# Values of the strided attention groups: token order and a DRAM round trip in place of a stationary operand of every fourth column

## The chip, the cores and the metric

The kernel runs on one core of a Trainium2 chip. TensorE (PE) multiplies, with a queue of its own for loading the stationary operand (PEld); VectorE (DVE), ScalarE (ACT) and GpSimd (POOL) do the elementwise work, and SyncE (SP) issues nearly all transfers. The metric is the device time of one execution in microseconds. Before the change it is 3572.5 us, the median of three runs between 3571.23 and 3573.5 us.

## The reference

The program is a stack of four layers over 512 tokens of 1024 features (with 256 context tokens in the first two), all in float32: a neighbourhood attention layer, a gated scan layer, and two hybrid layers, which the change touches. A hybrid layer projects the normed tokens to queries, keys and values of three attention groups of four heads (head size 128), to a retention branch and to gates. Group 0 attends the last 128 tokens; groups 1 and 2 attend tokens at distances that are multiples of 4 and of 16:

```python
ATT_PATTERNS = ((128, 1), (512, 4), (2048, 16))
...
def dilated_window_attention(q, k, v, window, dil):
    """Keys are gathered by stride: the sequence is split into dil residue classes, each attended with a
    banded (current + previous block) causal window."""
...
    def to_sub(t):
        t = t.astype(jnp.float32).reshape(B, L, dil, G, Dh).transpose(0, 2, 3, 1, 4)
```

The groups' outputs are weighted by their softmax denominators, gated, merged with the retention branch and projected back.

## The kernel before, in words

Every float32 product is made of three float32r products (`mm3`, L142 to L148): the operands are cut into a high and a low part, and high x high, high x low and low x high are added in PSUM. Weights come as 512 KB tiles `wraw` (three buffers, L121), which SP loads; a pair of tiles `whi`, `wlo` (six buffers each) holds 512 columns' worth of parts, the high ones made by ACT (L132), the low ones by POOL and DVE in turn (L135). A chunk of 256 weight columns for all 1024 input features is 1 MB: two `wraw` tiles, four pairs.

In a hybrid layer (`b2_layer`, L1360) `H` holds the normed tokens as two parts with features on the partitions. `dense` (L1322) gives 128 columns for all tokens with the weights stationary (128 x 512 outputs). `dense_v` (L1330) gives values, with tokens on the partitions: the tokens' parts are stationary and 256 weight columns move (128 x 256 outputs). It goes token tile after token tile; a tile takes 8 row blocks x 3 = 24 products, a call 96. With `classes`, for groups 1 and 2, tile `t` is made of every fourth token from `t` on, and the stationary operand is taken with that stride:

```python
            for k in range(KT):
                lh = [x[:, t::4] for x in H.row(k)] if classes else H.tok(k, t)
                S.mm3(p[:, u * 256:(u + 1) * 256], lh, W(k), k == 0, k == KT - 1)
```

So the stationary columns are 16 bytes apart. Two calls with `classes` follow each other ahead of heads 0 and 2 of each hybrid layer, for groups 1 and 2 of two heads at once: eight calls, 768 products. A call without `classes` stands in the retention's values (`b2_retain`, four a layer, with `parts`) and in group 0's for heads 2 and 3. ACT copies each pair of token tiles from PSUM to `V` (L1351).

`b2_attend` (L1411) then makes the queries and keys of what groups are left, the scores and exponentials, exchanges maxima and sums between the two token orders by way of DRAM (`stats`, L1455 and L1456), makes the first products of the next head (`between`), and then the outputs: probabilities are transposed (`pt`, L1480), copied (`PT`), and multiplied by `V` (`o`, L1494), first group 0 (`lay` 0), then groups 1 and 2. These last instructions lie between products of the next head in TensorE's order. A scheduler that works from priorities and modelled costs sets the order on each engine; each engine works its list in that order, and SP waits in its list for a buffer to come free.

Of the kernel before, what the change touches and what calls it, by code (L numbers as in the profile page):

```python
# [9 lines left out]
F32 = mybir.dt.float32  # L10
# [4 lines left out]
AF = mybir.ActivationFunctionType  # L15
# [3 lines left out]
D = 1024  # L19
KT = 8  # L20
# [5 lines left out]
KBASE = (0, 8, 24, 32)          # first key column of each 16-column query block  # L26
BOFF = (16, 8, 8, 0)            # its offset in the wide bias table
BVAR = (0, 1, 1, 2)

# columns of the packed per-feature vectors  # L30
# [10 lines left out]
# 2 pi in parts of 8 bits, whose products with small integers are exact  # L41
# [12 lines left out]
class Acts:  # L54
    """Activations with features on the partitions, as float32r parts [hi, lo]: 512 latent tokens and,
    in smaller tiles, 256 context tokens."""
# [18 lines left out]
class Prog:  # L75
# [14 lines left out]
    # ---------------------------------------------------------------- helpers  # L90
# [8 lines left out]
    def t2(self, name="t", n=512, dt=F32):  # L99
        """a short-lived tile of up to 2 KB a partition"""  # L100
        return self.sb.tile([128, n], dt, name=name, tag="t2", bufs=6)
# [7 lines left out]
    def weights(self, srcs, kt, own=None):  # L109
        """Loads float32 columns and cuts each value into two float32r parts whose sum it is.  # L110
        Returns a function of the row block that gives the two parts."""
# [27 lines left out]
    def wcols(self, w, c0, n, k0=0, kt=KT):  # L139
        """[128, kt, n] view of columns c0.. of a [K, N] weight."""  # L140
        return w[k0 * 128:(k0 + kt) * 128, c0:c0 + n].rearrange("(k p) n -> p k n", p=128)

    def mm3(self, out, lh, rh, first, last):
        """out (+)= (lh0+lh1).T @ (rh0+rh1), the product of the low parts being below float32."""
        nc = self.nc
        nc.tensor.matmul(out, lh[0], rh[0], start=first, stop=False)  # L146
        nc.tensor.matmul(out, lh[0], rh[1], start=False, stop=False)  # L147
        self.lastmm = nc.tensor.matmul(out, lh[1], rh[0], start=False, stop=last)  # L148

    def rsqrt(self, ss, scale, n, name="rs"):  # L150
        """(ss*scale + EPS) ** -0.5 on a few columns: Newton's steps from a first guess by the exponent."""
# [11 lines left out]
    def row_rstd(self, x, room):  # L163
        """(mean of squares + EPS) ** -0.5 of the rows of a token tile, half a row at a time; room: for the squares"""
# [12 lines left out]
    def rstd(self, ss, n, d):  # L177
        """(ss / d + EPS) ** -0.5 of sums of d squares, by GpSimd"""
# [6 lines left out]
    # ---------------------------------------------------------------- constants  # L185
    def setup(self):
# [11 lines left out]
        # the gated scan's lower bounds of the forget gates, and one less them  # L198
# [6 lines left out]
        # silu of the three conditioning vectors; c and c_ctx interleaved for the first products  # L205
# [7 lines left out]
    # ---------------------------------------------------------------- modulation vectors  # L213
    def ada_first(self):
        """shift and scale of the first norm for c and c_ctx, as columns: A = g * (1 + scale), shift"""
# [68 lines left out]
def ffn(S, l, xs, xout, more):  # L284
    """xout(t) is the residual tile that gets gate * swiglu(h); the last two of six tiles are the context's"""
# [16 lines left out]
    def dense(f):  # L302
        """a and u columns of feature tile f"""
# [18 lines left out]
    for gi, gn in enumerate(groups):  # L322
        gts = []
        for f in range(f0, f0 + gn):
# [5 lines left out]
            if l == 0:      # from columns first to rows first  # L330
# [12 lines left out]
            # a gate that this layer itself waits for comes at once  # L343
# [58 lines left out]
# which 1024 columns of a modulation matrix, and the names its vectors go by  # L402
# [3 lines left out]
def gemv_jobs(S, pool, wname, layer, part, vecs, ps, tag):  # L406
    """vec @ w + b for one 1024-column part, 256 columns a step, as a row in DRAM: S.rows[part, layer, v]."""
# [35 lines left out]
def gemv_rows(S, pool, wname, layer, part, ps, tag):  # L443
    """The same for c and c_ctx on the tensor engine, where other work leaves it idle."""
# [33 lines left out]
def gemv_flush(S, pool, ps, tag, after):  # L478
    """the sums over the partitions of the steps so far, behind other products so that no engine waits for them"""
# [21 lines left out]
def gate_bcast(S, part, layer, v, pool=None, tag="gate", bufs=2):  # L501
    """a modulation row on every partition"""
# [6 lines left out]
def mod_cols(S, sh, sc, g, layer, v):  # L509
    """(g * (1 + scale), shift) as columns"""  # L510
# [10 lines left out]
def residual_add(S, x, p, gate, c0, n):  # L521
    """x[:, c0:c0+n] += gate * p"""
# [6 lines left out]
def out_product(S, w, tok, xs, gates, own, tags, after=None):  # L529
    """xs[t] += gate * (h @ w): the first half of the columns for all the token tiles at once, row block by row  # L530
    block; then the other half a token tile after the other"""
# [25 lines left out]
def norm_block(S, xs, A, sh, rows, room, banks, hold=(), both=False, split=True):  # L557
    """h = x / rms(x) * A + sh of token tiles as two parts, with features on the partitions; rows(k): where
    row block k goes; room(): space for the scaled rows of a tile; banks: tags of the PSUM tiles to turn it in"""
# [43 lines left out]
def grid_rows(ap, t):  # L603
    """rows of a [512, D] array for the token tile of grid columns 16t.., column-major"""
# [16 lines left out]
def l0_start(S):  # L621
    nc, sb, ps, I = S.nc, S.sb, S.ps, S.I
    # residual rows, column-major grid order for the latent tokens
# [20 lines left out]
def na_heads(S, na, hT, jobs):  # L644
    """Head pair after head pair. The order of the instructions is the one they are written in: three phases of
    the attention, each a step behind the one before, with the products of the next heads between them."""
# [45 lines left out]
    # the products of the first heads come before the attention  # L692
# [63 lines left out]
class Feed:  # L756
    """A sequence of products, and of what follows from them some time of products later."""
# [8 lines left out]
    def then(self, lag, fn, cost=0.0):  # L766
        """after the last product and lag"""
# [11 lines left out]
def feed_weights(S, F, src, me):  # L779
    """the parts of a weight chunk, two row blocks at a time, as soon as the last one's products let them go"""  # L780
# [140 lines left out]
def o_row(oT, pr, lat):  # L921
    """outputs of a head pair, [feature, token]"""
# [5 lines left out]
def split_rows(S, oR, oT, pr):  # L928
    """the outputs of a head pair as two parts"""
# [7 lines left out]
def na_scores(S, na, st, g, h, b, qk, mask):  # L937
    """a step of the attention: softmax of 16 columns' queries, or of 128 context tokens"""
# [24 lines left out]
def na_max(S, me, h, b):  # L963
    """minus the maxima; the scores are negative ones"""
# [62 lines left out]
# ---------------------------------------------------------------- gated scan layer  # L1027
# [3 lines left out]
def view(t, off, dims):  # L1031
    """free-dimension pattern over a tile"""
# [80 lines left out]
def hg_qg(S, hT, w, c0, tag):  # L1113
    """silu of two heads' 256 columns from c0 on"""
# [16 lines left out]
def hg_head(S, hT, w, h, V, lb, om, masks, q, reads):  # L1131
# [4 lines left out]
    # forget gates; index 0 is the backward direction in f, the forward one in K  # L1136
# [26 lines left out]
    # Q: q (1 - lb) times the decays; the keys stay without their (1 - lb)  # L1163
# [10 lines left out]
    for li, m in enumerate(LEVELS):  # L1174
# [9 lines left out]
        # decays over whole blocks join  # L1184
# [19 lines left out]
    # states between the 128-token blocks: keys with tokens on the partitions, then k.T @ v  # L1204
# [41 lines left out]
def hg_read(S, h, on, g):  # L1246
    """output of a head, normed and gated, [feature, token]"""
# [16 lines left out]
# ---------------------------------------------------------------- hybrid layers  # L1264
# [3 lines left out]
def b2_tables(S):  # L1268
    """attention masks, and cos and sin of the rotary angles, [angle, position]"""
# [52 lines left out]
def dense(S, W, H, j):  # L1322
    """features on the partitions: 128 columns of a weight chunk for all the tokens"""
# [6 lines left out]
def dense_v(S, W, H, classes=False, parts=False, rows=False):  # L1330
    """tokens on the partitions: 256 columns of a weight chunk as [token, tile, column]; classes: tile r
    holds every fourth token from r on; parts: as two parts; rows: row block by row block"""
    V = [S.sb.tile([128, 4, 256], F32R if parts else F32, name="V", tag="hC", bufs=4) for _ in range(1 + parts)]
    if rows:
# [426 lines left out]
```

## Time and profile before

| What | Value |
|---|---|
| Median of three runs | 3572.5 us (3571.23 to 3573.5) |
| Span of the profiled execution | 3573.2 us |
| Mean granted TensorE clock | 0.990 |
| PE busy, share of the span | 3460.9 us, 97% |
| PEld busy | 2928.4 us, 82% |
| DVE, ACT, POOL busy | 1963.4, 1254.8, 717.7 us |
| HBM read, written | 324.16 MB, 8.54 MB |

The time that the profile gives for its own execution is the span; nothing further is recorded around it, and it lies 0.7 us over the median and inside the runs shown. Busy time of an engine counts its instructions' own durations. Products overlap, so the distance between two starts, not the duration of one, tells what a product costs in a row of them.

### The profile page before, as it was taken

Reading aid. Unit: us, or ns where it says so; the run is one execution under the profiler, and the core shown is the slowest. Engines: PE = TensorE matmul, PEld = TensorE weight load, DVE = VectorE, ACT = ScalarE, POOL = GpSimd, SP = SyncE. Lnnn points to the kernel's source line nnn. Section 1 sums busy time; section 2 is a strip of 40 time slices with the busy share of each in tenths; the row PEclk is TensorE's granted clock in tenths of the full one; section 3 lists DMA queues with packets and bytes.
Section 4 is the critical chain, followed back from the end, with each engine's and each line's share of the span. In section 5 each row is a group of like instructions: output and inputs, shape, how many; then the busy total and the mean of one; then the engine's idle time right before and its main releaser. Section 6 shows DMA issues by size and latency. Waiting matters only on the chain.

```text
span 3573.2 us, 49417 instructions
## 1 busy us (share of the span) xinstructions
PE 3460.9 (97%) x18796; PEld 2928.4 (82%) x18796; DVE 1963.4 (55%) x3910; ACT 1254.8 (35%) x2472; POOL 717.7 (20%) x651
## 2 busy tenths in 40 slices
PE   7999999999999899999999999999999999999999
PEld 5988857788778788887877888988888888888887
DVE  6566655847875566577787452336542413255523
ACT  4454534222222433334323243333333433333332
POOL 2112212111111301112222221111222311112122
PEclk9999999999999999999999999999999999999999
DMA  6121153423552211112565332222223322222332
GB/s 199 45 59 49 54 165 106 131 61 106 160 151 68 60 36 60 48 48 77 167 196 174 96 97 79 66 77 72 83 87 103 130 65 77 71 72 90 91 101 98
DMA packets 444734, 336.92 MB, mean 94 GB/s; under 512 B 39968, under 2 KB 417104, under 8 KB 444496
## 3 DMA queue, kind: packets, MB, share of 16 engines
q1 hardware_dynamic: 444064, 333.36, 31.1%
q8 instruction: 147, 2.41, 0.3%
q0 software_dynamic: 432, 0.41, 0.1%
q14 instruction: 91, 0.75, 0.1%
HBM read 324.16 MB, written 8.54 MB: 93 GB/s over the span
## 4 chain that ended last, share of the span: by engine, by line
PE 83%; DVE 9%; DMA 4%; ACT 2%; issue 2%; POOL 1%; SPq 0%; DVEq 0%; ACTq 0%; POOLq 0%
PE pacc L146 15%; PE pacc L147 15%; PE pacc L148 15%; PE pau L148 3%; PE pau L146 3%; PE pau L147 3%; PE po L146 2%; PE po L148 2%; PE po L147 2%; DVE gacc L432 2%; PE po L1017 2%; PE pw L148 2%; PE pw L146 2%; PE pw L147 2%; DMA araw<-ada_w 2%
## 5 line engine op out<-in xcount | busy, mean ns | idle before, releaser
L135 POOL TENSOR_TENSOR wlo<-wraw,whi 128x512 fp32r<-128x512 f32 x388 | 524.8, 1355 | 2227.8 <-ACT whi L132 2034.7
L132 ACT ACTIVATE whi<-wraw 128x512 fp32r<-128x512 f32 x776 | 483.6, 631 | 817.2 <-PE pacc L147 354.0
L135 DVE TENSOR_TENSOR wlo<-wraw,whi 128x512 fp32r<-128x512 f32 x388 | 323.6, 835 | 627.0 <-ACT whi L132 625.2
L146 PE MATMUL pacc<-hT,whi 128*128 128x512 f32 x1344 | 534.0, 397 | 0.0
L148 PE MATMUL pacc<-hT,wlo 128*128 128x512 f32 x1344 | 533.5, 397 | 0.0
L147 PE MATMUL pacc<-hT,whi 128*128 128x512 f32 x1344 | 531.9, 396 | 0.0
L146 PE MATMUL pacc<-whi,hT 128*128 128x256 f32 x1056 | 340.0, 322 | 4.0 <-DVE h L593 2.6
L147 PE MATMUL pacc<-wlo,hT 128*128 128x256 f32 x1056 | 331.0, 314 | 0.0
L148 PE MATMUL pacc<-whi,hT 128*128 128x256 f32 x1056 | 330.0, 313 | 0.0
L148 PEld LDWEIGHTS pacc<-hT,wlo 128*128 128x128 f32 x1344 | 253.4, 189 | 56.6
L147 PEld LDWEIGHTS pacc<-hT,whi 128*128 128x128 f32 x1344 | 253.4, 189 | 55.3
L146 PEld LDWEIGHTS pacc<-hT,whi 128*128 128x128 f32 x1344 | 253.6, 189 | 53.5
L148 PE MATMUL pau<-hT,wlo 128*128 128x512 f32 x704 | 281.7, 400 | 4.2 <-DVE wlo L135 4.2
L146 PE MATMUL pau<-hT,whi 128*128 128x512 f32 x704 | 281.7, 400 | 1.9 <-ACT whi L132 1.2
L147 PE MATMUL pau<-hT,whi 128*128 128x512 f32 x704 | 280.6, 399 | 0.0
L432 DVE SCALAR_TENSOR_TENSOR gacc<-araw,cact,gacc 128x256 f32<-128x256 f32 x448 | 249.4, 557 | 31.1 <-DMA araw<-ada_w 13.8
L146 PEld LDWEIGHTS pacc<-whi,hT 128*128 128x128 f32 x1056 | 237.6, 225 | 11.9 <-issue 5.5
L147 PEld LDWEIGHTS pacc<-wlo,hT 128*128 128x128 f32 x1056 | 238.0, 225 | 1.2 <-DVE wlo L797 0.3
L148 PEld LDWEIGHTS pacc<-whi,hT 128*128 128x128 f32 x1056 | 237.8, 225 | 0.0
L146 PE MATMUL po<-whi,gh 128*128 128x512 f32 x440 | 176.9, 403 | 15.3 <-ACT gh L340 14.4
L147 PE MATMUL po<-wlo,gh 128*128 128x512 f32 x440 | 175.1, 399 | 0.0
L148 PE MATMUL po<-whi,gl 128*128 128x512 f32 x440 | 174.7, 399 | 0.0
(366 smaller groups left out, 6623.2 us busy)
## 6 DMA issues: line engine op xcount, KB each, us to landing
araw<-ada_w SPq DMA_DIRECT2D x96, 512.0 KB
wraw<-w_in SPq DMA_DIRECT2D x96, 512.0 KB
wraw<-ffn_w_in SPq DMA_DIRECT2D x176, 256.0 KB
wraw<-w_in SPq DMA_DIRECT2D x160, 256.0 KB
araw<-w_ada SPq DMA_DIRECT2D x48, 512.0 KB
wraw<-ffn_w_out SPq DMA_DIRECT2D x40, 512.0 KB
x<-x SPq DMA_DIRECT2D x24, 512.0 KB
wraw<-hg_w_in SPq DMA_DIRECT2D x24, 512.0 KB
```

The lines of the kernel that those rows point to most:

```text
L132: nc.scalar.activation(hi, r, AF.Copy)
L135: eng.tensor_sub(lo, r, fr(hi))
L146: nc.tensor.matmul(out, lh[0], rh[0], start=first, stop=False)
L147: nc.tensor.matmul(out, lh[0], rh[1], start=False, stop=False)
L148: self.lastmm = nc.tensor.matmul(out, lh[1], rh[0], start=False, stop=last)
L432: nc.vector.scalar_tensor_tensor(acc, r, cv, acc, op0=OP.mult, op1=OP.add)
L1017: nc.tensor.matmul(po, v[:, vc:vc + 64], me["pT"][:, j, :], start=(j == 0), stop=(j == len(vv) - 1))
```

## The change

`dense_v` with `classes` computes tiles of 128 tokens in a row. ACT copies them to `vn`, a tile of the pool `x4`, SP writes each half (256 KB) to a DRAM tile of 512 rows of 256 values, and reads the whole (512 KB) back into `V`, four rows in a row to a partition, so that `V[0][j, r]` holds token 4j + r as before. The rest of the diff takes comments out and moves later lines down by 14.

```diff
 def dense_v(S, W, H, classes=False, parts=False, rows=False):
     V = [S.sb.tile([128, 4, 256], F32R if parts else F32, name="V", tag="hC", bufs=4) for _ in range(1 + parts)]
+    if classes:
+        d = S.dr.tile([LAT, 256], F32, name=f"v_{S.nstat}")
+        S.nstat += 1
+        vn = S.x4(name="vn").rearrange("p (t c) -> p t c", t=4)
+        for t2 in range(2):
+            p = S.acc()
+            for u in range(2):
+                for k in range(KT):
+                    S.mm3(p[:, u * 256:(u + 1) * 256], H.tok(k, 2 * t2 + u), W(k), k == 0, k == KT - 1)
+            sl = slice(2 * t2, 2 * t2 + 2)
+            S.nc.scalar.activation(vn[:, sl, :], p.rearrange("p (a b) -> p a b", a=2), AF.Copy)
+            S.nc.sync.dma_start(d[256 * t2:256 * t2 + 256, :].rearrange("(t p) c -> p t c", p=128), vn[:, sl, :])
+        S.nc.sync.dma_start(V[0], d.rearrange("(j r) c -> j r c", r=4))
+        return V[0]
...
             for k in range(KT):
-                lh = [x[:, t::4] for x in H.row(k)] if classes else H.tok(k, t)
-                S.mm3(p[:, u * 256:(u + 1) * 256], lh, W(k), k == 0, k == KT - 1)
+                S.mm3(p[:, u * 256:(u + 1) * 256], H.tok(k, t), W(k), k == 0, k == KT - 1)
```

The order of instructions on PE, ACT, DVE and POOL stays as it was, product for product. SP's list changes. At the start of the first hybrid layer it read, from the value weights (`128x4x256`) over the queries' and keys' (`128x4x128`) to the gate's (`128x8x128`) and the exchange of `stats`:

```order
L1280 DMA pos<-positions 128x512
L122 DMA wraw<-w_in 128x4x256 x3
L122 DMA wraw<-w_in 128x4x128 x12
L122 DMA wraw<-w_in 128x8x128
L122 DMA wraw<-w_in 128x4x128 x12
L1455 DMA stats_22049<-stats 128x4x2
```

Now the same stretch reads (`vn` are the copied tiles, `v` the DRAM tiles):

```order
L122 DMA wraw<-w_in 128x4x256 x3
L122 DMA wraw<-w_in 128x4x128 x4
L1346 DMA v_21463<-vn 128x2x256
L122 DMA wraw<-w_in 128x4x128
L1346 DMA v_21463<-vn 128x2x256
L122 DMA wraw<-w_in 128x4x128 x3
L1347 DMA V<-v_21463 128x1024
L1346 DMA v_21589<-vn 128x2x256
L122 DMA wraw<-w_in 128x4x128
L1346 DMA v_21589<-vn 128x2x256
L122 DMA wraw<-w_in 128x4x128 x3
L1347 DMA V<-v_21589 128x1024
```

Two writes and a read a call now stand between the loads of the queries' and keys' weights, and each write holds up what is behind it until ACT has copied its tiles.

TensorE's list gains waits at one place of each pair of calls, the first products of groups 1 and 2 with their values. It read, in the first hybrid layer:

```order
L148 MATMUL pacc<-hT,wlo 128x512
L1494 MATMUL o<-PT,V 128x128 [waits Activation_49]
L1494 MATMUL o<-PT,V 128x128 x3
L1480 MATMUL pt<-idf,P 128x128 [waits PE_49]
L1480 MATMUL pt<-idf,P 128x128 x3
```

It now reads (`o` by `V` is L1508, the transposes L1494):

```order
L148 MATMUL pacc<-hT,wlo 128x512
L1508 MATMUL o<-PT,V 128x128 [waits DMAHW1_49,Activation_49]
L1508 MATMUL o<-PT,V 128x128 [waits DMAHW0_49]
L1508 MATMUL o<-PT,V 128x128 x2
L1494 MATMUL pt<-idf,P 128x128 [waits PE_49]
L1494 MATMUL pt<-idf,P 128x128 x3
```

The first of these products waits for the read into the first `V`, the second for that into the other; what followed them follows still.

## Rows read from the trace of the kernel before

**Rows 1.** The page: busy time of each engine, and the granted clock by slices.

```profile
PE 3460.9 (97%) x18796; PEld 2928.4 (82%) x18796; DVE 1963.4 (55%) x3910; ACT 1254.8 (35%) x2472; POOL 717.7 (20%) x651
...
PEclk9999999999999999999999999999999999999999
```

**Rows 2.** The page: the chain that ended last, by engine.

```profile
PE 83%; DVE 9%; DMA 4%; ACT 2%; issue 2%; POOL 1%; SPq 0%; DVEq 0%; ACTq 0%; POOLq 0%
```

**Rows 3.** Waits of PE from 2110 to 3350 us, the two longest in total.

```profile
PE pt L584 <- DVE xn L568: 2.3, 1, 2.3
PE pv L146 <- ACT hT L589: 0.5, 1, 0.5
```

**Rows 4.** Groups by line, 2116.4 to 2139.1 us: a strided call, PE, then PEld.

```profile
L147 PE MATMUL pacc<-wlo,hT 128*128 128x256 f32 x32 | 12.8, 399 | 0.0
L147 PEld LDWEIGHTS pacc<-wlo,hT 128*128 128x128 f32 x32 | 10.7, 333 | 0.0
```

**Rows 5.** The same, 2492.5 to 2504 us: a call in token order.

```profile
L147 PE MATMUL pacc<-wlo,hT 128*128 128x256 f32 x32 | 9.1, 284 | 0.0
L147 PEld LDWEIGHTS pacc<-wlo,hT 128*128 128x128 f32 x32 | 6.0, 188 | 0.0
```

**Rows 6.** Timeline of ACT: copies of strided values, both layers (start, duration).

```profile
2139.30 0.60 ACT L1351 ACTIVATE V<-pacc 128x512 f32<-128x512 f32 x1 [0.74 <-PE pacc L148]
2150.66 0.60 ACT L1351 ACTIVATE V<-pacc 128x512 f32<-128x512 f32 x1 [10.24 <-PE pacc L148]
2162.02 0.60 ACT L1351 ACTIVATE V<-pacc 128x512 f32<-128x512 f32 x1 [0.74 <-PE pacc L148]
...
2872.83 0.60 ACT L1351 ACTIVATE V<-pacc 128x512 f32<-128x512 f32 x1 [0.72 <-PE pacc L148]
2884.03 0.60 ACT L1351 ACTIVATE V<-pacc 128x512 f32<-128x512 f32 x1 [10.08 <-PE pacc L148]
2895.23 0.60 ACT L1351 ACTIVATE V<-pacc 128x512 f32<-128x512 f32 x1 [0.72 <-PE pacc L148]
```

**Rows 7.** Timeline of ACT: copies of values in token order.

```profile
2498.42 0.60 ACT L1351 ACTIVATE V<-pacc 128x512 fp32r<-128x512 f32 x1 [2.08 <-PE pacc L148]
2504.18 0.60 ACT L1351 ACTIVATE V<-pacc 128x512 fp32r<-128x512 f32 x1
```

**Rows 8.** Windows (length, busy, PEclk, DMA share, GB/s): half clock; a strided call.

```profile
2107.20:2110.20 3.00, 3.00 (x16) 3.00 (x16) 3.00 (x3) 0.00 (x0) 3.00 (x3) 0.50 0.56 175
2120.00:2123.00 3.00, 3.00 (x14) 3.00 (x14) 2.93 (x5) 0.00 (x0) 0.00 (x0) 1.00 0.17 50
```

**Rows 9.** Timeline of PEld in the window of half clock, a load in token order.

```profile
2108.17 0.33 PEld L147 LDWEIGHTS pv<-wlo,hT 128*128 128x128 f32 x1
```

**Rows 10.** Windows: strided calls among 42 other products (first, third); such a call unstrided.

```profile
2289.70:2317.20 27.50, 27.50 (x142) 27.50 (x140) 6.14 (x9) 5.05 (x10) 2.20 (x3) 1.00 0.13 38
2434.00:2450.80 16.80, 16.80 (x142) 16.48 (x141) 9.45 (x15) 5.67 (x11) 1.83 (x2) 1.00 0.22 63
3023.40:3050.80 27.40, 27.40 (x141) 27.40 (x140) 6.13 (x9) 5.02 (x10) 2.12 (x3) 1.00 0.13 37
```

**Rows 11.** Timeline: splitting of weights near the end of a strided call.

```profile
2135.09 0.63 ACT L132 ACTIVATE whi<-wraw 128x512 fp32r<-128x512 f32 x1 [6.55 <-PE pacc L148]
2135.80 1.27 POOL L135 TENSOR_TENSOR wlo<-wraw,whi 128x512 fp32r<-128x512 f32 x1 [19.53 <-ACT whi L132]
```

**Rows 12.** Timeline of SP and ACT: a 512 KB load from issue to first use.

```profile
2106.63 0.38 SPq L122 DMA_DIRECT2D wraw<-w_in  x1
2110.25 0.63 ACT L132 ACTIVATE whi<-wraw 128x512 fp32r<-128x512 f32 x1 [3.50 <-DMA wraw<-w_in]
```

**Rows 13.** Timeline of SP: a write to DRAM and the read that waits for it.

```profile
2207.07 0.37 SPq L1455 DMA_DIRECT2D stats<-stats  x1
2210.01 0.34 SPq L1456 DMA_DIRECT2D stats<-stats  x1
```

**Rows 14.** Timeline of ACT and PE: last copy for heads 2, 3; first products of heads 0, 2.

```profile
2340.08 0.60 ACT L1351 ACTIVATE V<-pacc 128x512 f32<-128x512 f32 x1 [0.74 <-PE pacc L148]
...
2234.12 0.41 PE L1494 MATMUL o<-PT,V 128*128 128x128 f32 x2
2389.99 0.51 PE L1494 MATMUL o<-PT,V 128*128 128x128 f32 x3
```

**Rows 15.** Windows: the densest transfers near the first strided call.

```profile
2111.00:2116.00 5.00, 5.00 (x44) 5.00 (x43) 4.86 (x7) 1.64 (x4) 2.79 (x3) 1.00 0.68 208
```

**Rows 16.** The page: the queue of SP's transfers (packets, MB, share of 16 engines).

```profile
q1 hardware_dynamic: 444064, 333.36, 31.1%
```

## The prediction, as put on record

> **What bounds the kernel now.** I read the page first: TensorE is busy 97% of the span at full granted clock in nearly every slice [rows 1], and the chain that ended last runs through it for 83% [rows 2]. The waits of PE over both hybrid layers say the same: the longest in total is 2.3 us [rows 3]. So in these layers the end moves with what TensorE's own instructions cost, and a change pays if the products get cheaper and nothing comes to wait. Next I set two calls of `dense_v` side by side in the groups by line: the strided call and the one in token order, with the same operations, shapes and counts. The reader is to see that one load of the stationary operand takes 333 ns in the strided call [rows 4] and 188 ns in the other [rows 5], and a product 399 ns against 284 ns.
>
> Durations overlap, so the price of a product is taken from ACT's copies of finished tiles. Between two of them lie 48 products, 2 token tiles x 8 row blocks x 3. In the first hybrid layer they stand 11.36 us apart, 236.7 ns a product; in the second 11.20 us, 233.3 ns [rows 6]. In token order it is 5.76 us, 120.0 ns [rows 7]. The granted clock is full in the strided stretch: the profile also shows a stretch at half clock, 1.2 GHz, where loads in token order take 0.33 us too [rows 9], but the strided call has 1.00 in the clock's column [rows 8]. So the stride is what differs.
>
> **The change, part by part.**
>
> *The products.* All 768 strided products become products in token order, with the same instructions in the same places of TensorE's list. Six of the eight calls are free of other work. In the first layer such a call gains 96 x (236.7 - 120.0) ns = 11.2 us; there are two for heads 0 and 1 and one for heads 2 and 3. In the second layer the two calls for heads 0 and 1 gain 96 x (233.3 - 120.0) ns = 10.9 us each, and for the last, whose pace I take as the first layer's, 11.2 us. The two others, the first call for heads 2 and 3 of each layer, hold 42 products of the attention before. With these they last 27.5 and 27.4 us; a call in token order with the same number of products in its window lasts 16.8 us [rows 10], and that one already pays for TensorE's waits for copied probabilities, which a faster stream covers less. So they gain 10.7 and 10.6 us. Without such waits it would be 11.2; I take the measured pair. The sum: 11.2 + 11.2 + 10.7 + 11.2 + 10.9 + 10.9 + 10.6 + 11.2 = 87.9 us.
>
> *Weight parts.* Two calls in token order directly behind each other are new. There are six buffers of parts and four pairs a call, so the third pair of a call waits for the first buffer of the call before. That buffer is let go after 6 of the last tile's 24 products, 18 x 0.12 = 2.2 us before the call's end, and it is needed 12 x 0.12 = 1.4 us into the next: 3.6 us for ACT's 0.63 us and POOL's 1.27 us [rows 11]. I take nothing, with 1.7 us to spare. If handing over ate that cover, each pair of calls would lose at most those 1.9 us once, 7.6 us in all.
>
> *Copies.* ACT copies as many tiles as before, 0.60 us each [rows 6], only to another place: nothing.
>
> *SP's list.* Every call adds two writes of 256 KB and a read of 512 KB, 24 transfers in all. An issue takes 0.34 to 0.38 us on SP [rows 12, 13], which only matters for what queues behind. The second write of a call waits for the copy of its last tiles, some 1 us after the call's end; three loads of queries' and keys' weights stand right behind it. One of these, issued about 1.4 us after the end, is ready 3.6 us later [rows 12], at 5 us. It is due when a part buffer falls free in the next call's last tile, 11.5 - 2.2 = 9.3 us after the end. So 4 us of cover hide it. The read waits for the write; the nearest row, a small write to DRAM and the read behind it, has 2.9 us between the issues [rows 13], so it goes out at 4 to 5 us and is past before the next call's first write, which waits until 5.8 us plus a copy. I take nothing; both ends: nothing, and one exposed load of 3.6 us a call, 29 us in all.
>
> *Transfer rate.* In the eight calls 2 MB move where 1 MB did, in half the time: 2.1 MB in 11.5 us is 182 GB/s. The densest stretch near by moved 208 GB/s with the DMA engines 68% busy [rows 15]. So it fits, with transfers longer than those I timed; that is why I keep the upper end above.
>
> *The wait added to TensorE.* The first products of groups 1 and 2 now wait for the reads, and the next head's products are queued behind them. The round trip ends about 1 + 3.6 + 3.6 = 8 us after the call, a write at most as slow as a load of 512 KB. From the last copy to these products there are 72 us for heads 0 and 1 [rows 6, 14] and 50 us for heads 2 and 3 [rows 14], and nothing between gets shorter by the change. Nothing, then.
>
> The profiled execution took 3573.2 us, 0.7 us over the median of 3572.5. 3573.2 - 87.9 = 3485.3, against the median 3484.6; I say **3485 us**.
>
> **The rivals.**
>
> *A. The gain is partly given back to weights that come late.* In the two calls TensorE takes weights twice as fast as before, while SP's list makes loads wait for copies and the DMA engines carry twice the bytes. For it: three loads stand behind each second write, and the calculated cover of 4 us is about one transfer. Against it: the chunks in token order elsewhere eat weights at the same pace and TensorE waits for none of them [rows 3]. With one load of 3.6 us exposed in each of the eight calls the time is 3485 + 29 = 3514 us.
>
> *B. The layout of the stationary operand costs nothing, and nothing changes.* Loads would take their time by the number of columns, and what the strided calls show would come from where they stand. Against it: all calls of both kinds are in the same layers, at full clock, with the same second operand, and the pace differs by a factor of 1.97 [rows 6, 7]. The time would be the old one, 3572 us. Two sentences of the Trainium skill stand on this side. "TensorE: Matmul & The Clock Gate", section "LDWEIGHTS (loading the stationary operand)", prices a load by its columns alone, which makes 128 / 1.2 = 107 ns of either kind and a gain of zero. "SBUF — State Buffer", section "Door 1: The DMA port swizzle", speaks of 16-byte lines and says that one can stride for free over 4 fp32, which, if it means a step of four values as here, is no gain either; the same passage asks for two hits a line, which this stride misses. The trace disagrees with a free stride: 333 against 188 ns.
>
> *C. Slower: the round trip comes too late.* The place is the wait of TensorE for `V`, with the next head's products behind it. It decides once the round trip takes longer than the 50 us of cover for heads 2 and 3 and the 22 us that this pair of calls gains, 72 us in place of 8. That needs small packets. The queue's 444064 packets took 31.1% of 16 engines' span [rows 16], 0.311 x 16 x 3573.2 / 444064 = 0.040 us each; a last write and a read that take 36 us apiece have 36 x 16 / 0.040 = 14400 packets, 36 bytes each. If the reordering went value by value, 131072 packets a transfer, each would take 328 us, four to a pair of calls 1311 us, some 1250 beyond the cover, and the kernel about 3485 + 4 x 1250 = 8500 us. Against it: the write's rows are 256 values, 1 KB, and the read takes four DRAM rows in a row, 4 KB a partition.
>
> **How the numbers follow.** The forecast, the full gain with small change either way, gets 0.84; A 0.12; B 0.03; C 0.01. Downward there is little room: with 119 ns a product the gain grows by 0.8 us, the half-clock stretch ahead of the first strided call [rows 8] costs some 1.5 us and need not come again, and the runs scatter by 1.2 us: 3481. Upward the range takes in the 7.6 us of the part buffers (3493) and somewhat over half of A: 3502. A measurement of this kernel can tell 0.2%, 7 us, from no change. Faster by more than that holds in the forecast and in A, 0.96; B is the same, 0.03; C slower, 0.01.
>
> **What would show it.** All loads of the stationary operand in the values' calls near 188 ns, no second population at 333, and copies to `vn` 5.7 to 5.8 us apart where no other work lies between. The 22.7 us calls become 11.5, the 27.5 us ones about 16.8. Among the waits of PE none at `o` ends with a read into `V`. PE's busy time falls by about 88 us, and its share stays near 97%. HBM reads and writes grow by 4.2 MB each, 8 x 512 KB. For A one would see ACT's high parts waiting for `wraw` in or behind the calls, and TensorE for parts; for B the same load times as now; for C a wait at `o` released by the transfer into `V`. The prediction is wrong if the loads get short and the calls don't, or if the calls get short and the span falls by much less than 80 us.

## The result and the profile after

The changed kernel takes **3487.1 us** (median of 4 runs, 3485.5 to 3491.2) against 3572.4 us for the kernel before in the same session (4 runs, 3571.2 to 3573.5): a ratio of 0.9761, 95% interval 0.9747 to 0.9775. The prediction was 3485 us with a range of 3481 to 3502. The span of the profiled execution is 3487.0 us where it was 3573.2: 86.2 us less.

The page of the changed kernel, the lines that answer to [rows 1], [rows 2] and [rows 16], has TensorE's busy time first, then the granted clock by slices, SP's queue, HBM, and the chain that ended last:

```profile
PE 3379.6 (97%) x18796; PEld 2844.1 (82%) x18796; DVE 1970.5 (57%) x3910; ACT 1255.3 (36%) x2472; POOL 721.6 (21%) x651
...
PEclk9999999999999999999999999999999999999999
...
q1 hardware_dynamic: 449568, 341.75, 32.7%
...
HBM read 328.36 MB, written 12.74 MB: 98 GB/s over the span
...
PE 84%; DVE 8%; DMA 3%; ACT 2%; issue 2%; POOL 1%; SPq 0%; DVEq 0%; POOLq 0%; ACTq 0%
```

The instructions on PE are as many as before. Its busy time is 81.3 us shorter, and its share and the chain are what they were: nothing else has become the bound. HBM reads and writes are each 4.2 MB more, the round trips.

The groups by line of the first call that was strided (2117.4 to 2128.8 us) answer to [rows 4]:

```profile
L147 PE MATMUL pacc<-wlo,hT 128*128 128x256 f32 x32 | 9.0, 281 | 0.0
...
L147 PEld LDWEIGHTS pacc<-wlo,hT 128*128 128x128 f32 x32 | 6.0, 188 | 0.0
```

A load has come down from 333 to 188 ns and a product from 399 to 281 ns, close to [rows 5] (188 and 284). In all eight calls the loads lie near 188 ns; none near 333 is left. The timeline of ACT shows the pace, against [rows 6]; the columns are start, duration, engine, line:

```profile
2129.03 0.60 ACT L1345 ACTIVATE vn<-pacc 128x512 f32<-128x512 f32 x1
...
2134.72 0.60 ACT L1345 ACTIVATE vn<-pacc 128x512 f32<-128x512 f32 x1 [4.58 <-PE pacc L148]
...
2140.42 0.60 ACT L1345 ACTIVATE vn<-pacc 128x512 f32<-128x512 f32 x1
```

The copies are 5.69 and 5.70 us apart where they were 11.36: 48 products at 118.6 ns. The windows of that call and of one with 42 other products in it (columns: length, then busy time and instructions of PE, PEld, DVE, ACT and POOL, PEclk, DMA share, GB/s) answer to [rows 8, 10]:

```profile
2117.40:2128.80 11.40, 11.40 (x98) 11.40 (x97) 8.60 (x15) 4.38 (x9) 1.15 (x1) 1.00 0.39 116
2268.20:2285.10 16.90, 16.90 (x141) 16.45 (x140) 6.00 (x9) 4.86 (x10) 1.59 (x2) 1.00 0.25 74
```

Taken from the start of its first product to the start of the next other product, the eight calls went as follows (us):

| Call | before | after | gained | forecast |
|---|---|---|---|---|
| Layer 1, heads 0/1, both | 22.72 each | 11.39 each | 22.66 | 22.4 |
| Layer 1, heads 2/3, first (42 other products) | 27.41 | 16.87 | 10.54 | 10.7 |
| Layer 1, heads 2/3, second | 22.71 | 11.39 | 11.32 | 11.2 |
| Layer 2, heads 0/1, both | 22.40 each | 11.52 each | 21.76 | 21.8 |
| Layer 2, heads 2/3, first (42 other products) | 27.39 | 16.87 | 10.52 | 10.6 |
| Layer 2, heads 2/3, second | 22.72 | 11.39 | 11.33 | 11.2 |
| Sum | | | 88.1 | 87.9 |

The waits of PE over both hybrid layers, from 2080 to 3280 us, answer to [rows 3]. That window begins 30 us earlier, so that it also holds the first layer's norm (total, times, longest):

```profile
PE pt L584 <- DVE xn L568: 5.8, 2, 3.4
PE pv L147 <- DVE wlo L135: 2.3, 1, 2.3
PE pv L146 <- ACT hT L589: 0.8, 2, 0.5
```

They lie in the two norms and ahead of the first values. None is at `o` for a read into `V`, and none in the calls for parts of weights. SP's timeline around the first two calls shows how close the round trip follows:

```profile
2127.07 0.37 SPq L1346 DMA_DIRECT2D v<-vn  x1
2129.55 0.37 SPq L122 DMA_DIRECT2D wraw<-w_in  x1
2129.97 0.50 SPq L1346 DMA_DIRECT2D v<-vn  x1
2130.52 1.89 SPq L122 DMA_DIRECT2D wraw<-w_in  x3
2133.71 0.34 SPq L1347 DMA_DIRECT2D V<-v  x1
...
2144.83 0.34 SPq L1347 DMA_DIRECT2D V<-v  x1
```

The first call ends at 2128.83 us. Its second write goes out 1.1 us later, the three loads behind it begin 1.7 us after the end, and the read goes out 3.7 us after the write; the second call ends at 2140.2 us, and its read goes out 4.6 us later.

### The profile page after: what moved, and what is told of

Its sections match the earlier page's. It is cut to its first block, busy times and chain, and to the rows that moved or that the text cites. A ratio compares the mean times of both kernels' runs of the same rounds, so it can differ in the third digit from the quotient of the medians.

```text
span 3487.0 us, 49457 instructions
## 1 busy us (share of the span) xinstructions
PE 3379.6 (97%) x18796; PEld 2844.1 (82%) x18796; DVE 1970.5 (57%) x3910; ACT 1255.3 (36%) x2472; POOL 721.6 (21%) x651
## 3 DMA queue, kind: packets, MB, share of 16 engines
q1 hardware_dynamic: 449568, 341.75, 32.7%
## 4 chain that ended last, share of the span: by engine, by line
PE 84%; DVE 8%; DMA 3%; ACT 2%; issue 2%; POOL 1%; SPq 0%; DVEq 0%; POOLq 0%; ACTq 0%
PE pacc L146 15%; PE pacc L148 14%; PE pacc L147 14%; PE pau L148 3%; PE pau L146 3%; PE pau L147 3%; PE po L146 3%; PE po L148 3%; PE po L147 3%; PE po L1017 2%; DVE gacc L432 2%; PE pw L148 2%; PE pw L146 2%; PE pw L147 2%; DMA araw<-ada_w 2%
## 5 line engine op out<-in xcount | busy, mean ns | idle before, releaser
L146 PE MATMUL pacc<-whi,hT 128*128 128x256 f32 x1056 | 310.6, 294 | 3.9 <-DVE h L593 2.5
L147 PE MATMUL pacc<-wlo,hT 128*128 128x256 f32 x1056 | 301.0, 285 | 0.0
L148 PE MATMUL pacc<-whi,hT 128*128 128x256 f32 x1056 | 300.1, 284 | 0.0
L146 PEld LDWEIGHTS pacc<-whi,hT 128*128 128x128 f32 x1056 | 201.0, 190 | 11.9 <-issue 5.5
L147 PEld LDWEIGHTS pacc<-wlo,hT 128*128 128x128 f32 x1056 | 201.7, 191 | 1.2 <-DVE wlo L797 0.3
L148 PEld LDWEIGHTS pacc<-whi,hT 128*128 128x128 f32 x1056 | 200.9, 190 | 0.0
```

## The experiments

My theory: the stride of the stationary operand is the whole price, and the round trip lies under cover. The rivals are that the trip, or the other order of SP's list, carries part of the result; and, for the stride, that something other than the distance of 16 bytes sets the price.

### One half of the change at a time

`e1_no_trip` takes token order without the round trip:

```diff
-    vs = lambda h, g: dense_v(S, ..., H, classes=(g > 0),
+    vs = lambda h, g: dense_v(S, ..., H, classes=False,
```

> Left out: the values of the two strided groups stay in token order, they are neither written to DRAM nor read back. Theory (the stationary stride is the whole price, the round trip is hidden): the time of the changed kernel within 4 us, 3483 to 3491 us, and the two calls for heads 0 and 1 last 11.4 to 11.5 us each, as with the round trip. Rival (the round trip takes back part of the gain, by transfers or by the loads that SP holds behind it): clearly shorter than the changed kernel; 3.6 us in each of the eight calls would make it 3458 us.

Measured: 3483.8 us (4 runs, 3480.4 to 3489.4), ratio to the kernel before 0.9748, interval 0.9731 to 0.9764, which overlaps the change's own. The pairs of calls for heads 0 and 1 last 23.2 and 22.8 us.

`e2_stride_trip` does the round trip with the old stationary operand:

```diff
-                    S.mm3(p[:, u * 256:(u + 1) * 256], H.tok(k, 2 * t2 + u), W(k), k == 0, k == KT - 1)
+                    S.mm3(p[:, u * 256:(u + 1) * 256], [x[:, 2 * t2 + u::4] for x in H.row(k)], W(k), k == 0,
+                          k == KT - 1)
```

> The round trip of the changed kernel with the strided stationary operand of the one before (so these values are reordered twice). Theory: the time of the kernel before within 4 us, 3569 to 3577 us, loads of the stationary operand at 333 ns in the eight calls, which last 22.4 to 22.7 us where nothing lies between. Rival 1 (what makes the changed kernel faster is something that came with the round trip, such as the copies going to another tile): near 3487 us. Rival 2 (the round trip costs, and the gain of 88 us is net of it): up to 3.6 us a call more, 3601 us.

Measured: 3574.1 us (10 runs), ratio 0.9997, interval 0.9988 to 1.0006; the calls last 22.4 and 22.7 us, and 27.4 among other products, as before. So the stride alone carries the 86 us. The trip costs nothing that these runs can tell, with either pace of products: without it the median is 2 to 3 us lower, well inside the intervals.

### What about the stride costs

`e3_steps` leaves the round trip out and gives each of the eight calls a step of its own between stationary columns (in float32 values, so four bytes each):

```diff
+STEPS = [2, 3, 1, 5, 6, 8, 4, 16]
...
+        step = STEPS.pop(0)
...
+                    lh = [view(x, k * 256 + 2 * t2 + u, ([step, 128],)) for x in H.lat]
+                    S.mm3(p[:, u * 256:(u + 1) * 256], lh, W(k), k == 0, k == KT - 1)
```

> No round trip, and each of the eight calls takes its stationary operand at another step between columns (so these values come from wrong tokens and row blocks): 2, 3, 1, 5, then 6, 8, 4, 16 values in the order of the program; the third and the seventh lie among 42 other products. Theory (a load is slowed where a column no longer shares a 16-byte line with its neighbour): step 2 costs nothing, 119 to 120 ns a product and 11.4 to 11.5 us a call; step 3, with three of four columns on a new line, lies between; 4, 5, 6, 8 and 16 all cost the same, 233 to 237 ns and 22.4 to 22.7 us. The time is then 3485 + 8 for step 3 + 4 x 11.2 + 10.5 = 3549 us. Rival 1 (the price grows with the step): 8 near 470 ns and 45 us, 16 near 940 ns and 90 us, about 3660 us. Rival 2 (the fourfold step meets one bank of a memory of several, and uneven steps escape): 3 and 5 as cheap as 1, 8 and 16 at least as dear as 4, about 3530 us.

Measured: 3545.0 us in one run, near the 3549 expected; the call at step 3 lasts 16.9 us where 19.4 were expected. The windows of 10 us inside the eight calls (columns as above), in the order 2, 3, 1, 5, 6, 8, 4, 16; the third and seventh hold products of the attention too:

```profile
2116.00:2126.00 10.00, 10.00 (x85) 10.00 (x85) 7.68 (x14) 2.97 (x6) 0.02 (x1) 1.00 0.37 107
2129.00:2139.00 10.00, 10.00 (x59) 10.00 (x59) 0.52 (x1) 0.60 (x1) 0.00 (x0) 1.00 0.36 104
2276.00:2286.00 10.00, 10.00 (x86) 9.76 (x85) 3.46 (x5) 1.83 (x3) 0.00 (x0) 1.00 0.03 9
2292.00:2302.00 10.00, 10.00 (x46) 10.00 (x45) 0.00 (x0) 0.60 (x1) 0.00 (x0) 1.00 0.26 75
2825.00:2835.00 10.00, 10.00 (x45) 10.00 (x46) 0.00 (x0) 0.60 (x1) 0.00 (x0) 1.00 0.18 51
2848.00:2858.00 10.00, 10.00 (x43) 10.00 (x43) 0.00 (x0) 0.60 (x1) 0.00 (x0) 1.00 0.06 18
3008.00:3018.00 10.00, 10.00 (x44) 10.00 (x43) 0.96 (x2) 1.23 (x2) 0.00 (x0) 1.00 0.00 0
3026.00:3036.00 10.00, 10.00 (x47) 10.00 (x46) 0.00 (x0) 0.60 (x1) 0.00 (x0) 1.00 0.17 49
```

In 10 us TensorE does some 85 products at step 2, as at step 1; 59 at step 3; and 43 to 47 at every step from 4 to 16. So the price does not grow with the step beyond 4, and the powers of two 8 and 16 stand on both sides of the odd step 5: the two rivals fall. The steps sort by how many columns share 16 bytes: two or more (steps 1 and 2) at the low price, one (4 and above) at the full one, step 3 between. They would sort alike by the bare distance between columns (8 bytes cheap, 16 dear, and no dearer beyond), and these steps don't tell the two apart. The loads go with it, in the groups by line of the calls with step 3, 5 and 8:

```profile
L147 PEld LDWEIGHTS pacc<-wlo,hT 128*128 128x128 f32 x20 | 5.2, 262 | 0.0
...
L147 PEld LDWEIGHTS pacc<-wlo,hT 128*128 128x128 f32 x15 | 4.8, 319 | 0.0
...
L147 PEld LDWEIGHTS pacc<-wlo,hT 128*128 128x128 f32 x14 | 4.7, 339 | 0.0
```

The page "SBUF — State Buffer" of the Trainium skill, section "Door 1: The DMA port swizzle", speaks of 16-byte lines that want two accesses each, and with that these runs agree. With its next clause, that one strides free over 4 fp32, they disagree if it means a step of four: step 4 pays the full price, and free ends at 2.

### Hiding the load in place of removing it

`e7_wide_stride` keeps the strided operand, takes no round trip, and makes groups 1 and 2 in one call, so that 512 weight columns move past each load; the copies stay apart by group. The row blocks then form the outer loop, and all four token tiles are open at once, two of them in PSUM tiles of the scores (`s`):

```diff
+            lh = [x[:, t::4] for x in H.row(k)] if stride else H.tok(k, t)
+            S.mm3(ps[t], lh, W(k), k == 0, k == KT - 1)
...
-            V += [vs(h, g) for g in (1, 2)]
+            V += dense_wide(S, S.weights([S.wcols(w, VA + g * 512 + h * 128, 256) for g in (1, 2)], KT), H, True)
```

> The strided stationary operand, no round trip, but both strided groups in one call: 512 weight columns move past each stationary operand in place of 256, so that a pair of calls issues 96 products and loads in place of 192 and computes the same values. Theory (a strided load occupies its queue for 237 ns, and a product of 512 columns, which takes 233 ns in the kernel's dense calls, covers that): 96 x 0.237 = 22.7 us a pair, as much as the 22.8 us of two calls in token order, so 3483 to 3493 us with loads still at 333 ns. Rival (a strided load slows the product itself, or cannot run beside a longer product): 96 x (0.233 + 0.117) = 33.6 us a pair, about 3530 us; or no gain, 3572 us, if a product's time doubles with it.

Measured: 3488.3 us (4 runs, 3487.0 to 3490.0), ratio 0.9757, interval 0.9743 to 0.9772: the change's own gain, with neither token order nor a round trip. Its window, and the loads in it from the groups by line:

```profile
2118.00:2136.00 18.00, 18.00 (x76) 18.00 (x76) 10.30 (x16) 5.53 (x10) 4.42 (x4) 1.00 0.40 117
```

```profile
L147 PEld LDWEIGHTS pacc<-wlo,hT 128*128 128x128 f32 x14 | 4.4, 311 | 0.0
```

A load still takes 311 ns, and PEld is busy throughout; but the products, 237 ns each (18.00 / 76), carry twice the columns, so that 96 are wanted where the two strided calls took 192.

`e6_wide` does the same in token order, with the round trip (the edit above without its last argument, and two writes and two reads a pair).

> Token order and the round trip as in the changed kernel, but both strided groups in one call with 512 moving columns, 96 products in place of 192 a pair of calls. Theory: a product of 512 columns takes 233 ns and one of 256 takes 119 to 120, so a pair lasts 22.4 in place of 22.8 to 23.0 us, 2 us in all four: 3481 to 3488 us, not to be told from the changed kernel. Rival (the products of the 256-column calls are held by their loads even in token order, so wider ones pay): more than 7 us shorter, below 3480 us.

Its window over the same stretch:

```profile
2118.00:2136.00 18.00, 18.00 (x79) 14.62 (x78) 7.61 (x10) 6.35 (x11) 5.05 (x4) 1.00 0.41 119
```

Measured: 3483.0 us (4 runs, 3476.7 to 3483.3), ratio 0.9742, interval 0.9727 to 0.9756, against 0.9754 (0.9739 to 0.9768) for the changed kernel again, in the same session:

> The changed kernel as it is, for its spread beside the others. Theory: the median lies within 3 us of 3487 us, and its executions differ by whole stretches of half clock in TensorE's clock: with one stretch of 3.4 us more, an execution is 1 to 2 us longer. Rival: executions of equal granted clock differ as much as those of unequal, so the scatter comes from the round trip's transfers.

That one had 3486.0 us (4 runs), within 3 us of 3487 as expected; its scatter is taken up in the last section. In the wide form, whose window stands above, PEld is idle for 3.4 of 18 us, and a pair lasts 22.3 to 22.4 us where two calls last 22.8 to 23.0 (among other products 27.5 to 27.6 where they last 28.3). In sum that is some 2.6 us, near the 2 us of the expectation, but the two intervals overlap: it is not told apart from the change, and single runs of `e5_four_trips` and `e9_pieces16` below lie as low.

### How much round trip the cover holds

Each of these three adds trips through DRAM behind the first, one, three and nine of them; they write `V` out and read it back:

```diff
+        for i in range(1):
+            e = S.dr.tile([LAT, 256], F32, name=f"e{i}_{S.nstat}")
+            S.nc.sync.dma_start(e.rearrange("(j r) c -> j r c", r=4), V[0])
+            S.nc.sync.dma_start(V[0], e.rearrange("(j r) c -> j r c", r=4))
```

> One further write of the reordered values to DRAM and read back behind each of the eight calls, in SP's list at the same place (the values are the same). Theory: the round trip has cover to spare on TensorE's side (42 us or more) and some 4 us in SP's list; the further trip holds SP to about 12 us after a call's end, where the next loads fall due, so 3485 to 3492 us. Rival (the one round trip of the changed kernel already uses up the cover of the loads): 3.6 us or more in each call, 3516 us and above.

Measured: 3484.1 us (4 runs, 3482.1 to 3486.2), ratio 0.9747, interval 0.9731 to 0.9763: no cost that these runs can tell.

> Three further round trips behind each of the eight calls, one after the other in SP's list (the values are the same). Theory: SP is then held to about 27 us after a call's end, some 15 us past the time when the next loads fall due, and TensorE runs out of weights: with 4 us of cover about 11 us a call, 3575 us; the wait shows at the weights' parts, not at the products with V. Rival (what has to be covered is only the way of V to its first use, 42 us or more, and four trips take 8 + 22 = 30 us): 3487 us, no wait.

Measured: 3482.0 us in one run. **My theory fell here.** I had taken SP to be held by the trips' waits, and weights to come late. The waits of SP from 2115 to 2200 us are there, but the scheduler put loads of weights between the trips, and SP's timeline has them in turn:

```profile
SPq L1351 <- DMA e<-V: 12.6, 6, 3.3
...
SPq L1350 <- DMA V<-v: 5.0, 2, 3.7
```

```profile
2147.08 0.32 SPq L1350 DMA_DIRECT2D e<-V  x1
2148.74 0.32 SPq L1351 DMA_DIRECT2D V<-e  x1
2149.16 0.41 SPq L122 DMA_DIRECT2D wraw<-w_in  x1
...
2165.78 0.34 SPq L1351 DMA_DIRECT2D V<-e  x1
```

A trip's wait holds SP for 3.7 us at most, less than the 4 us of cover that I had given the weights. The second call ends at 2133.4 us and the last read goes out at 2165.8 us, well inside the 72 us of cover for heads 0 and 1. The rival held here: with three trips more, only the way of `V` to its first use wants cover.

> Nine further round trips behind each of the eight calls (the values are the same); the scheduler puts loads of weights between them, as it did with three. With three, the last read landed some 36 us after the pair's second call, 8.5 us a trip. Theory (what has to be covered is the way of V to its first use, 72 us for heads 0 and 1 and 50 us for heads 2 and 3): nine end some 87 us after the call, 15 and 37 us late, so 3485 + 2 x (15 + 37) = 3589 us, and TensorE's wait shows at the products with V. Rival 1 (the price shows at the weights, which wait in the same list): a wait of TensorE at the weights' parts, of any size. Rival 2: no wait, 3485 us.

Measured: 3528.4 us in one run, 42 us above the repeated change (3486.0) where about 103 were expected. So the cover does end, as expected, but my size was well over twice too large. PE's longest waits from 2080 to 3300 us, and the window of the first pair of heads:

```profile
PE pt L1498 <- DVE P L1496: 9.6, 4, 3.2
PE s L146 <- ACT P L1465: 7.4, 6, 2.1
PE o L1512 <- DMA V<-e: 6.7, 4, 2.4
```

```profile
2138.00:2230.00 92.00, 84.40 (x389) 68.66 (x388) 31.33 (x78) 30.47 (x67) 17.53 (x14) 0.96 0.92 287
```

SP's timeline in that window has the exchange of `stats` among the trips, its write and the read that waits for it:

```profile
2187.05 0.45 SPq L1473 DMA_DIRECT2D stats<-stats  x1
...
2192.59 0.32 SPq L1474 DMA_DIRECT2D stats<-stats  x1
```

Waits at `o` for the last read into `V` have come, but they make 6.7 us. The larger ones stand at the scores and the transposed probabilities: the exchange of `stats` now queues in SP's list between the trips (5.5 us from its write to its read, 2.9 in [rows 13]), and the DMA engines are 92% busy. Against the profile of the repeated change TensorE is idle for 30.9 us more and busy for 11.7 us more, and half clock is in that (0.96 in the window). What the trips' data, the exchange and the clock are each worth of the 42 us I did not separate.

### Small pieces

Rival C priced a packet of any size at 0.040 us. `e9_pieces16` sends the round trip in pieces of 64 bytes, `e10_pieces4` in pieces of 16, both with the same bytes; the edit also makes four writes and four reads a call of 128 KB each, in place of two and one:

```diff
-        d = S.dr.tile([LAT, 256], F32, name=f"v_{S.nstat}")
+        d = S.dr.tile([16, LAT, 16], F32, name=f"v_{S.nstat}")
...
+                S.nc.sync.dma_start(d[:, 128 * t:128 * t + 128, :].rearrange("a p b -> p a b"),
+                                    vn[:, t, :].rearrange("p (a b) -> p a b", b=16))
...
```

> The round trip in pieces of 16 values, 64 bytes, in place of rows of 1 KB: the DRAM tile is laid out so that neither the writes nor the reads find longer runs (the values are the same). Theory (a packet costs about 0.04 us of one of 16 engines whatever its size, so 512 KB take 20 us, and four such transfers a pair stand before or among the weights' loads): the loads come up to 16 us late a pair and V just in time, 3520 to 3560 us, with TensorE's wait at the weights' parts. Rival (small packets cost in proportion to their bytes): 3485 us, no wait.

Measured: 3479.9 us in one run: nothing lost that can be told. **The flat price fell.** The page's line for SP's queue:

```profile
q1 hardware_dynamic: 576160, 341.75, 34.7%
```

Against 449568 packets and 32.7% of the changed kernel that is 126592 packets more for 0.347 x 16 x 3478.1 - 0.327 x 16 x 3487.0 = 1066 us of the 16 engines together, about 0.01 us each.

> The round trip in pieces of 4 values, 16 bytes (the values are the same). Theory (0.04 us a packet on 16 engines): 82 us for 512 KB, four of them a pair 328 us, against 50 to 72 us of cover and 23 us of the calls themselves: about 250 us late a pair, 4500 us, slower than the kernel before, with TensorE waiting for V or for weights behind it. Rival (in proportion to the bytes): 3485 us.

Measured: 4630.9 us in one run, slower than the kernel before, near my figure of about 4500 us. The queue's line for the whole span, then for 2125 to 2275 us (the first call's writes) and for 2280 to 2300 us (mostly its reads):

```profile
q1 hardware_dynamic: 969376, 341.75, 65.9%
```

```profile
q1 hardware_dynamic: 33890, 1.05, 159.8%
```

```profile
q1 hardware_dynamic: 34912, 0.59, 114.8%
```

Over the span a further packet has 0.06 us of packet time: 519808 more than in the changed kernel, for 0.659 x 16 x 4629.1 - 18244 = 30565 us. But packet times overlap here, more than 100% of 16 engines in both stretches, so the pace is the better price: 150 x 16 / 33890 = 0.07 us a packet while the pieces are written, 20 x 16 / 34912 = 0.01 us while they are read. As many pieces are written as read, and the mean of the two prices is 0.04: that 4500 us came near is luck, for the flat price is wrong for both.

PE's waits over the span, ACT's for the weights from 2100 to 2500 us, and SP's timeline behind the first call:

```profile
PE pacc L146 <- ACT whi L132: 409.3, 5, 140.4
PE pacc L146 <- ACT vn L1345: 363.7, 4, 132.7
PE pacc L146 <- DVE kl L1424: 300.3, 4, 141.8
```

```profile
ACT whi L132 <- DMA wraw<-w_in: 316.9, 6, 148.0
```

```profile
2195.40 39.77 SPq L1348 DMA_DIRECT2D v<-vn  x2
2235.21 35.95 SPq L122 DMA_DIRECT2D wraw<-w_in  x3
2279.59 13.85 SPq L1351 DMA_DIRECT2D V<-v  x4
```

SP needs 40 us to issue two writes of 128 KB and 36 us for the three loads of weights behind them, against 14 us for the four reads. TensorE stands at `pacc`, the products of queries and keys, not at `o`: with SP held by writes, the loads behind them go out and come late, and ACT's high parts wait for `wraw`, which is the sign that the prediction names for rival A. The engines that PE's rows name as releasers were long done when the waits ended; ACT's row shows that the loads of weights were not.

## Why the prediction held

*The products.* The sum was 87.9 us, the calls gained 88.1; every term came within 0.2 us of its call. Copies of finished tiles give 236.7 - 118.6 = 118.1 ns a product; durations say 399 - 281 = 118, so this case doesn't show that the one unit was needed in place of the other. Before the result the two stood at 116.7 and 115 ns. The choice to price the two mixed calls by a measured mixed call, and not by 96 x 116.7 ns, was right: they gained 10.5 us each, not 11.2.

*The span* fell by 86.2 us, 1.9 less than the calls gained, and PE's busy time by 81.3 where I had said about 88; its idle time fell by the other 4.9. Most of that exchange lies where the change does nothing: from 0 to 2085 us, ahead of the hybrid layers, TensorE is busy for 1996.3 us where it was 1992.3. For the 1.9 us one place shows a cause. The windows of the norm in the second hybrid layer, first in the kernel before and then after:

```profile
2780.00:2870.00 90.00, 86.95 (x434) 75.91 (x433) 35.58 (x43) 33.87 (x63) 27.15 (x29) 1.00 0.36 122
```

```profile
2780.00:2800.00 20.00, 17.38 (x100) 14.84 (x99) 9.64 (x13) 11.78 (x20) 5.15 (x7) 0.91 0.15 61
```

Before, TensorE had full clock throughout; now 0.91 over 20 us, half clock (1.2 GHz) for some 3.5 us behind a wait for `xn`, at most 1.8 us of work at full clock. The wait itself, 2.3 us, was there before [rows 3]. The prediction had one such stretch [rows 8] that might not come again; it did, and a second came. The rest is within what runs of one kernel differ by.

*The profiled execution's own time.* I took the span for it. In the runs since, an execution's time is 1.7 us above its span (3488.7 and 3487.0 here). So 3573.2 was a span to be set against 3487.0, not against a median of times: that it lay 0.7 us over the median says nothing of its own time. The forecast hardly hangs on this step, since the median gave 3484.6 and the span 3485.3, both 3485.

*Parts, copies, SP's list, rate.* Nothing, as forecast: no wait for parts in the calls, loads 1.7 us behind a call's end (forecast 1.4), read 4.6 to 4.9 us behind it (4 to 5). The rate fits too: 185 GB/s over the second call (2128.8 to 2140.2 us), where 182 were worked out.

*The added wait.* The forecast cover was never touched: one more trip and three more cost nothing, and with nine TensorE waits for `V`.

*The rivals.* A did not occur; `e10_pieces4` shows its wait once two writes hold SP for 40 us, where I had priced one transfer of 3.6 us. B is excluded by the loads in the calls, 188 where they took 333 ns, and by `e2_stride_trip`. C has the right sign, and two steps of it were wrong: "0.040 us each" for a packet, which is 0.01 at 64 bytes, and at 16 bytes 0.07 written and 0.01 read, and its place, which was to be the wait for `V` and is the weights behind the writes. Its limit of 36 bytes a packet lies between the two sizes tried.

## What to carry to other kernels

Before a layout is changed, set two calls side by side that differ in it alone, and price a product by the distance between finished tiles; then ask what could be late, and give each its cover. Where the stationary columns lie 16 bytes or more apart, look first whether more columns can move past each load: here that gave the same gain without token order or a round trip. And keep reordering through DRAM in pieces that SP's list can bear: what hurt most here, with pieces of 16 bytes and with nine trips more, was not the data's own arrival but what waited behind or between its transfers.

## What was not expected of the hardware

**Half clock goes with part of the scatter between runs.** Executions of the same instructions differ by several microseconds, and the longer ones tend to have the lower mean granted clock: the changed kernel and its near neighbours (`e1_no_trip`, `e4_two_trips`, `e5_four_trips`, `e9_pieces16`) had spans of 3478.1 to 3480.8 us at 0.991 in their profiles, 3484.1 and 3484.4 at 0.989, and 3487.0 at 0.988. The stretches at half clock follow waits of TensorE, as ahead of the hybrid layers' first products [rows 8], and are not the same in every execution. But runs at the same mean clock differ too: beside `e1_no_trip`, eight runs of the kernel before, all at 0.989, had spans of 3568.4 to 3576.2 us, while 0.001 of that span is 3.6 us of work at full clock. So executions of equal clock do differ, as the rival of `a0_after` has it; but the round trip is not the cause, for the kernel before has none and scatters as much. That the clock causes its part, and does not merely go with it, no run here isolates.

**A step of three is neither free nor dear:** 262 ns a load and 59 products in 10 us, between 85 at a step of two and 43 to 47 from four on.

**A packet of 64 bytes adds about 0.01 us; one of 16 bytes takes 0.01 us when it is read and 0.07 us when it is written,** by the pace of 16 engines in `e10_pieces4`: the first call's four writes take 150 us (2125 to 2275 us), its four reads, with the same bytes in the same pieces, 20 us.
